# A two-layer hybrid backbone on one core: loads asked for earlier and in rooms of their own in the up projections, and context tiles beside two products of the first down projection

## The chip, the cores and the metric

The kernel runs on 1 core of one Trainium2 chip. The metric is the device time of the core in microseconds (us); the time of the kernel before is the median of 3 runs. The engines are PE (TensorE, matmuls), DVE (VectorE), ACT (ScalarE), POOL (GpSimd) and SP (SyncE, from whose queue every DMA of this kernel is issued).

## The reference

1024 latent tokens and 256 context tokens of width 1024 go through two layers. Each layer has a mixer (attention in layer 0, a gated recurrence in layer 1) and a convolutional feed-forward part, each modulated by rows that come from a conditioning vector (`ada_w`). Only the feed-forward part and those rows matter here:

```python
def conv_ffn(h, w_up, conv_w, conv_b, w_down):
    g, v = jnp.split(dwconv_centred(h @ w_up, conv_w, conv_b), 2, axis=-1)
    return (jax.nn.gelu(g, approximate=True) * v) @ w_down

mod_lat = (jax.nn.silu(c) @ ada_w[l] + ada_b[l])[:, None, :]
x = layer_norm(alpha * x + g1 * o_lat, ln1_g[l], ln1_b[l])
f_lat = conv_ffn(x * (1.0 + sc2) + sh2, ffn_w_up[l], ffn_conv_w[l], ffn_conv_b[l], ffn_w_down[l])
x = layer_norm(alpha * x + g2 * f_lat, ln2_g[l], ln2_b[l])
if not last:   # the same for the 256 context tokens
    f_ctx = conv_ffn(ctx * (1.0 + csc2) + csh2, ffn_w_up[l], ...)
```

The hidden width is 2816 = 22 blocks of 128. In layer 1 the context isn't needed after the mixer.

## The kernel before

All matmuls take three passes (`mm3`, lines 130 to 132): both operands are split into a high part (a cast on ACT, line 109) and a low part (a subtraction on DVE or POOL, line 110). Several large products are done with seven half-size products instead of eight (Strassen-Winograd); p1 to p7 are their names in the code.

**Up projection** (`ffn_up`, line 951). It goes over 22 channel blocks j. From j=3 on each j has the items p1, p2, (cg), p6, p5, p7, p3, p4, (cv); cg and cv are the context tokens' products, in layer 0 only. The weights of a j are two tiles of 512 KB, loaded into the ring `wr` of three buffers and split by `quarters` (line 940 forms their sums on POOL), four items ahead of use. Results leave the banks by copies on ACT and adds on DVE (lines 1059, 1075, 1078), go through a convolution along the tokens (`conv`, lines 895 to 898), GELU, and the product of gate and value (line 1087), and are stored as `g_s[j]`.

Beside this, a generator `more` is advanced by one step per item (not for cg and cv). In layer 0, `beside` (line 1165) first forms modulation rows (`ada`, 32 tiles of `ada_w`, one per step, each loaded into the ring `wr` and reduced by one DVE instruction at line 212) and then sums of layer 1's down weights (`down_sums`, 22 pieces: two loads of `w_dn`, four DVE subtractions at lines 380 to 386, two stores to `tw_s`; a piece lies in one `wr` buffer). In layer 1 `beside` does nothing.

From j=11 on, sums of the hidden values for the down projection (`sa_s`) are formed too (`more_sums`, lines 1108 to 1114): at item p1 of the next j, `g_s[j-11]` is loaded into lane 4, which is also the lane of the value convolution, and the four operations follow at p6, p5 and p7.

**Down projection** (`down`, line 1174). `run` goes over k blocks: it loads and splits a block of hidden values and a block of weights and does 12 matmuls. Banks 0 to 3 are set A, 4 to 7 set B. In layer 0 the two context tiles come first, alone, over all 22 k with weights 1024 wide; then p1 (A), p2 (B), p6 (A, on top of p1), p5 (B), p3 (B), p7 (A, on top), p4 (A, on top), 11 k each. `put` multiplies by the gate row, `norm` is the layer norm of a row tile, `modulate` transposes the result for the next block, as steps between the matmuls of the next `run` (`left`, `chain`). `fetch` loads a row tile of the residual and applies two DVE passes (lines 1191, 1195).

The order on each engine is that of the program, with a scheduler that may move an instruction ahead where the program leaves it free; matmuls with a key (`pe_key`) keep the program's order. An instruction that waits holds all behind it on its engine; the SP queue is such an engine for DMAs.

Of the kernel before, what the change touches and what calls it, by code (L numbers as in the profile page):

```python
# [58 lines left out]
class Kernel:  # L59
# [132 lines left out]
    def ada(self, pool, jobs, b):  # L192
# [8 lines left out]
        self.ld(bias, self.a["ada_b"])  # L201
        for l, part in jobs:
# [148 lines left out]
    def down_sums(self, pool, l, n):  # L351
# [3 lines left out]
        todo = [(k, c) for k in range(HF) for c in range(0, 512, n)]  # L355
# [16 lines left out]
        while have:  # L372
            if pool is None:
                yield
            k, view, x, y = have.pop(0)
            if pool is not None and todo:
                fetch()
                yield
# [4 lines left out]
            if pool is not None:  # L383
                yield
# [4 lines left out]
            if todo and not have:  # L389
                fetch()  # L390
                yield
# [559 lines left out]
    def ffn_up(self, l, nt, left, plain, lanes, jobs=()):  # L951
# [19 lines left out]
        with ExitStack() as es:  # L971
            self.spare((6, 7))
            more = self.beside(jobs)
# [59 lines left out]
            def finish(at, j, i):  # L1033
# [59 lines left out]
                end = j == KF - 1 and i == ends(j)  # L1093
                if len(both) == 1 and (i == "p1" or end):
                    f = lane(4)
                    self.ld(f[:, :TL], self.g_s[j - HF - (not end), :, :TL])
                    both.append(f)
                if not end:
                    more_sums(j - HF - 1, i)

            def more_sums(k, i):

                if len(both) < 2 or i not in ("p6", "p5", "p7"):
                    return
                g, f = both
                a11, a21, a12, a22 = f[:, :512], f[:, 512:TL], g[:, :512], g[:, 512:TL]
                if i == "p6":
                    nc.vector.tensor_add(a22, a21, a22)  # L1108
                elif i == "p5":
                    nc.vector.tensor_sub(a21, a11, a21)  # L1110
                    nc.vector.tensor_sub(a11, a22, a11)
                    self.st(self.sa_s[l, k, 1], f[:, :TL])
                else:
                    nc.vector.tensor_sub(a12, a12, a11)
                    self.st(self.sa_s[l, k, 0], g[:, :TL])
                    both.clear()

            sums, made_sums = iter(()), 0
            both = []
            for at, (j, i) in enumerate(seq):  # L1120
# [31 lines left out]
                if at >= begin + 8 and i not in ("cg", "cv"):  # L1152
# [4 lines left out]
            def rest():  # L1157
                for i in ("p6", "p5", "p7"):
                    more_sums(KF - 1 - HF, i)
                    yield  # L1160
# [3 lines left out]
    def beside(self, jobs):  # L1164


        if not jobs:
            return
        with ExitStack() as es:
            yield from self.ada(self.pool(es, "up", 1), jobs, 6)  # L1170
        yield from self.down_sums(None, 1, 256)


    def down(self, l, nt, x_in, x_out, nx, fold, norm_in, rest):
# [91 lines left out]

        A, B = ([(self.banks(i + s), None, i) for i in range(H)] for s in (0, 4))
        g, sa, tw = self.g_s, self.sa_s[l], self.tw_s[l]
        r1, r2 = half(0), half(1)
        if nt > NTL:  # L1270
# [3 lines left out]
            run(acc, KF, lambda k: g[k, :, TL:], lambda k: w[k], True, True, tiles)  # L1274
# [5 lines left out]
        self.spare((6, 7))  # L1280
        run(A, HF, lambda k: g[k, :, r1], lambda k: w[k][:, r1], True, False)
        p1, p5 = ([kept(n, u) for u in range(H)] for n in ("p1", "p5"))
        for o, _, u in A:
            nc.scalar.copy(p1[u], o)
        run(B, HF, lambda k: g[HF + k, :, r1], lambda k: w[HF + k][:, r1], True, True)
        for o, _, u in B:
            nc.vector.tensor_add(p1[u], o, p1[u])
            put(u, 0, p1[u])
        run(A, HF, lambda k: sa[k, 1, :, r1], lambda k: tw[k, 1, :, r2], False, False)
        p1 = [kept("p1", u) for u in range(H)]  # L1290
        for o, _, u in A:
            nc.scalar.copy(p1[u], o)
        run(B, HF, lambda k: sa[k, 0, :, r2], lambda k: tw[k, 0, :, r1], True, True,
            range(H if fold is not None else NTL))
# [558 lines left out]
```

## Time and profile before

| | |
|---|---|
| median of 3 runs | 2876.4 us (2875.54 to 2880.41) |
| the profiled execution's own time | 2875.91 us |
| its span, first to last instruction | 2872.9 us |
| mean granted clock of PE | 0.985 of 2.4 GHz |
| PE busy | 2745.3 us, 96% |
| DVE busy | 2172.5 us, 76% |
| ACT busy | 1526.6 us, 53% |
| POOL busy | 774.7 us, 27% |
| DMA | 493.48 MB, mean 172 GB/s |

Busy times are sums over instructions, as shares of the span; matmuls are pipelined, so their spans overlap. A granted clock of 1 is 2.4 GHz, and where a row shows less, part of its time was granted half of that. In the trace, layer 0's up projections with seven products per j run from about 1011 to 1528 us, its down projection from about 1515 to 1803 us, the recurrent block after it, layer 1's up projections from about 2200 to 2659 us, and its down projection to the end.

### The profile page before, as it was taken

What the parts mean: (1) busy time and instruction counts of PE and PEld (TensorE: products, weight loads), DVE (VectorE), ACT (ScalarE), POOL (GpSimd) and SP (SyncE); (2) the same over time, 40 slices, a digit from 0 to 9 for tenths busy, and PEclk for the clock granted to TensorE, in tenths of its full rate; (3) what the DMA queues carried; (4) which work ended last, traced back from release to release, by engine and by line L of the source; (5) the groups of instructions that cost most, each with busy time, mean ns of one, the idle gap of its engine ahead of it and who ended that gap; (6) DMA issues with size and microseconds to landing.
All of it is one profiled execution on the core that took longest, in us unless ns stands there. A gap on an engine that the chain in (4) does not pass through costs nothing.

```text
span 2872.9 us, 39350 instructions
## 1 busy us (share of the span) xinstructions
PE 2745.3 (96%) x14246; PEld 2273.4 (79%) x14246; DVE 2172.5 (76%) x3088; ACT 1526.6 (53%) x2490; POOL 774.7 (27%) x635
## 2 busy tenths in 40 slices
PE   7999999999999998999999999999989999999997
PEld 4877888888877877777887888788767888877885
DVE  6469878876666988778867758588787977877677
ACT  4222257777767643344444545577757544444444
POOL 4000002332100043444530001343211367762002
PEclk9999999999999999999999999999999999999998
DMA  7886875446175145446548667211264122446764
GB/s 291 323 265 242 278 221 122 96 114 145 62 268 197 48 165 183 167 165 225 174 144 285 209 198 241 89 52 58 73 232 152 59 89 88 140 155 219 256 217 165
DMA packets 197252, 493.48 MB, mean 172 GB/s; under 512 B 20382, under 2 KB 68542, under 8 KB 196930
## 3 DMA queue, kind: packets, MB, share of 16 engines
q1 hardware_dynamic: 197058, 490.98, 52.0%
q8 instruction: 111, 1.82, 0.3%
q14 instruction: 83, 0.68, 0.1%
HBM read 365.31 MB, written 125.59 MB: 171 GB/s over the span
## 4 chain that ended last, share of the span: by engine, by line
PE 38%; DVE 8%; DMA 5%; issue 3%; ACT 3%; POOL 1%; SPq 0%; DVEq 0%; ACTq 0%; POOLq 0%
PE pb L131 13%; PE pb L132 13%; PE pb L130 13%; DMA lane<-g_s 2%; DVE lane L898 1%; DVE lane L896 1%; DMA x<-x_s 1%; DVE lane L1087 1%; DVE wq L110 1%; DMA ar<-g_s 1%; DMA tw<-w_dn 1%; ACT lane L895 1%; POOL sq L940 1%; POOL wq L110 0%; DVE lane L1108 0%
## 5 line engine op out<-in xcount | busy, mean ns | idle before, releaser
L130 PE MATMUL pb<-hh,wh 128*128 128x512 f32 (+1 forms) x704 | 256.6, 365 | 8.2 <-ACT wh L109 8.0
L131 PE MATMUL pb<-hl,wh 128*128 128x512 f32 (+1 forms) x704 | 257.1, 365 | 0.4 <-DVE hl L731 0.4
L132 PE MATMUL pb<-hh,wl 128*128 128x512 f32 (+1 forms) x704 | 255.7, 365 | 1.0 <-DVE wl L110 1.0
L130 PE MATMUL pb<-wq,a 128*128 128x512 f32 x616 | 241.6, 392 | 6.2 <-ACT a L109 2.8
L131 PE MATMUL pb<-wq,a 128*128 128x512 f32 x616 | 240.8, 391 | 0.0
L109 ACT CAST a<-ar 128x512 fp32r<-128x512 f32 (+2 forms) x224 | 129.1, 580 | 191.3 <-PE pb L132 156.6
L110 DVE TENSOR_TENSOR wq<-wr,wq 128x512 fp32r<-128x512 f32 x262 | 203.3, 778 | 34.7 <-ACT wq L109 19.4
L110 DVE TENSOR_TENSOR a<-ar,a 128x512 fp32r<-128x512 f32 (+2 forms) x224 | 143.6, 644 | 103.6 <-ACT a L109 101.8
L940 POOL TENSOR_TENSOR sq<-wr 128x512 f32<-128x512 f32 x72 | 127.2, 1767 | 325.3 <-DMA wr<-w_up 268.5
L109 ACT CAST wq<-wr 128x512 fp32r<-128x512 f32 x262 | 161.5, 618 | 99.8 <-PE pb L132 62.8
L708 POOL TENSOR_SCALAR s<-s 128x1 f32<-128x1 f32 x36 | 21.7, 603 | 711.8 <-ACT x L707 711.4
L132 PE MATMUL pb<-wq,a 128*128 128x512 f32 x616 | 211.1, 391 | 0.0
L110 POOL TENSOR_TENSOR wq<-sq,wq 128x512 fp32r<-128x512 f32 x96 | 161.5, 1690 | 122.6 <-ACT wq L109 122.6
L130 PE MATMUL pb<-t,wq 128*128 128x512 f32 x400 | 161.4, 404 | 21.4 <-DVE lane L1075 12.5
L568 ACT ACTIVATE p<-pb,nm 128x1280 f32<-128x1280 f32 (+3 forms) x160 | 159.4, 999 | 40.2 <-DVE nm L1558 34.6
L131 PE MATMUL pb<-t,wq 128*128 128x512 f32 x400 | 160.0, 400 | 0.0
L132 PE MATMUL pb<-t,wq 128*128 128x512 f32 x400 | 159.7, 400 | 0.0
L109 ACT CAST wh<-wr 128x1024 fp32r<-128x1024 f32 x91 | 95.5, 1050 | 120.5 <-DMA wr<-w_qk 44.3
L130 PEld LDWEIGHTS pb<-hh,wh 128*128 128x128 f32 x704 | 133.7, 190 | 29.5 <-ACT wh L109 8.2
L110 DVE TENSOR_TENSOR wl<-wr,wh 128x1024 fp32r<-128x1024 f32 x91 | 111.0, 1220 | 58.6 <-ACT wh L109 57.6
L896 DVE SCALAR_TENSOR_TENSOR lane<-lane,cv 128x1023 f32<-128x1023 f32 x88 | 123.6, 1406 | 39.9 <-ACT lane L895 39.7
L131 PEld LDWEIGHTS pb<-hl,wh 128*128 128x128 f32 x704 | 133.7, 190 | 22.6 <-DVE hl L731 1.4
(357 smaller groups left out, 8135.1 us busy)
## 6 DMA issues: line engine op xcount, KB each, us to landing
wr<-w_up SPq DMA_DIRECT2D x88, 512.0 KB, 3.6
wr<-ada_w SPq DMA_DIRECT2D x80, 512.0 KB, 4.1
sa_s<-lane SPq DMA_DIRECT2D x44, 512.0 KB, 3.4
wr<-tw_s SPq DMA_DIRECT2D x88, 256.0 KB, 4.3
ar<-sa_s SPq DMA_DIRECT2D x88, 256.0 KB, 2.9
wr<-w_dn SPq DMA_DIRECT2D x66, 256.0 KB, 3.2
ar<-g_s SPq DMA_DIRECT2D x66, 256.0 KB, 4.0
wr<-w_ao SPq DMA_DIRECT2D x32, 512.0 KB, 7.1
```

The costliest lines, as they stand in the source:

```text
L109: self.cast = self.nc.scalar.copy(h, raw)
L110: return (sub or self.nc.vector).tensor_sub(l, raw, h.bitcast(F32))
L130: i = mm(out, a[0], b[0], start=first, stop=False, **kw)
L131: mm(out, a[0], b[1], start=False, stop=False, **kw)
L132: j = mm(out, a[1], b[0], start=False, stop=last, **kw)
L568: self.in_turn("att_act", self.nc.scalar.activation(*args, **kw))
L708: nc.gpsimd.tensor_scalar(rs, sq, 1.0 / D, EPS, op0=ALU.mult, op1=ALU.add)
L895: nc.scalar.activation(c, u, AF.Identity, scale=cvw[:, 1:2], bias=cvw[:, 3:4])
L896: nc.vector.scalar_tensor_tensor(c[:, 1:], u[:, :n - 1], cvw[:, 0:1], c[:, 1:], op0=ALU.mult, op1=ALU.add)
L898: nc.vector.scalar_tensor_tensor(c[:, :n - 1], u[:, 1:], cvw[:, 2:3], c[:, :n - 1], op0=ALU.mult, op1=ALU.add)
L940: op(have[n], x, y)
L1087: nc.vector.tensor_mul(g[:, :n], c.pop((j, 0))[:, :n], c.pop((j, 1))[:, :n])
```

## The change

In `ada` (with `apart`), a tile is asked for before the tile ahead of it is used, and every second tile gives one step more, so two tiles take three steps. In `down_sums`, `gap` sets how many steps lie between a load and its use (3 in layer 0, 4 in layer 1), and 9 of the 22 pieces of layer 1's weights move from layer 0's to layer 1's up projections, where they use a buffer of their own (`room`) and not the ring. The tile `f` for `more_sums` gets that room too; it is asked for at p3 of the same j instead of p1 of the next, and the operations come at p2, p6 and p5. In layer 0's down projection the context tiles no longer run alone: over the first 11 k they go with p1 and use the same split weights, over the other 11 k with p6; then p7, p2, p5, p3 and p4 follow. Layer 1's order stays.

```diff
-    def ada(self, pool, jobs, b):
+    def ada(self, pool, jobs, b, apart=False):
...
             for k in range(KD):
-                w = self.ring.tile([P, D], F32, name="wr", tag="wr")
-                self.ld(w, self.a["ada_w"][l, part, k])
+                w = have.pop(0) if have else turned(l, part, k)
+                if apart:
+                    at = jobs.index((l, part)) * KD + k + 1
+                    if at < len(jobs) * KD:
+                        have.append(turned(*jobs[at // KD], at % KD))
+                    if k % 2:
+                        yield
...
-    def down_sums(self, pool, l, n):
+    def down_sums(self, pool, l, n, part=slice(None), gap=0):
...
-            if pool is None:
-                xy = self.ring.tile([P, 2, 2, n], F32, name="tw", tag="wr")
+            if gap:
+                xy = (pool or self.ring).tile([P, 2, 2, n], F32, name="tw", tag="room" if pool else "wr")
...
-            if pool is None:
+            for _ in range(gap - 1):
                 yield
...
             self.st(view(self.tw_s[l, k, 0]), x)
-            if pool is not None:
-                yield
+            yield
...
             yield
-            if todo and not have:
+            if gap and todo:
                 fetch()
                 yield
...
-                end = j == KF - 1 and i == ends(j)
-                if len(both) == 1 and (i == "p1" or end):
-                    f = lane(4)
-                    self.ld(f[:, :TL], self.g_s[j - HF - (not end), :, :TL])
-                    both.append(f)
-                if not end:
+                if j >= HF and i == ("p3" if j < KF - 1 else ends(j)):
+
+                    f = room().tile([P, TL], F32, name="f", tag="room") if i == "p3" else lane(4)[:, :TL]
+                    self.ld(f, self.g_s[j - HF, :, :TL])
+                    other.append(f)
+                if j > HF:
                     more_sums(j - HF - 1, i)
...
-                if i == "p6":
+                if i == "p2":
                     nc.vector.tensor_add(a22, a21, a22)
-                elif i == "p5":
+                elif i == "p6":
...
-                if at >= begin + 8 and i not in ("cg", "cv"):
+                if at >= begin + 9 and i not in ("cg", "cv"):
                     next(more, None)
...
-        if not jobs:
-            return
-        with ExitStack() as es:
-            yield from self.ada(self.pool(es, "up", 1), jobs, 6)
-        yield from self.down_sums(None, 1, 256)
+        if l == 0:
+            with ExitStack() as es:
+                yield from self.ada(self.pool(es, "up", 1), jobs, 6, True)
+            yield from self.down_sums(None, 1, 256, slice(0, 13), 3)
+        else:
+            yield from self.down_sums(room(), 1, 256, slice(13, None), 4)
...
+        def with_ctx(acc, ctx, k0, a, b, fresh, want=()):
...
+            self.pe_key = f"dn{l}"
+            for k in range(HF):
+                parts = []
+                for src, cols in ((g[k0 + k, :, TL:], TC), (a(k), 512)):
...
+                    self.ld(ar[:, :cols], src)
+                    self.split(ar[:, :cols], hl[:, :cols], hl[:, 512:512 + cols])
+                    parts.append((hl, hl[:, 512:]))
+                wc = self.weight(w[k0 + k], (P, D), nc.vector)
+                wm = [x[:, r1] for x in wc]
+                if b is not None:
...
+                    self.ld(raw, b(k))
+                    self.split(raw, wq[:, 0], wq[:, 1])
+                    wm = wq[:, 0], wq[:, 1]
...
+                work = [(parts[0], wc, ctx, k0 + k == 0, k0 + k == KF - 1),
+                        (parts[1], wm, acc, fresh and k == 0, False)]
+                for x, ws, sums_, start, end in work if k0 + k < KF - 1 else work[::-1]:
...
         if nt > NTL:
...
-            run(acc, KF, lambda k: g[k, :, TL:], lambda k: w[k], True, True, tiles)
+            with_ctx(A, acc, 0, product[1][2], None, True)
+            p1 = copies("p1", A)
+            with_ctx(A, acc, HF, product[6][2], product[6][3], False, tiles)
+            p6 = copies("p6", A)
             for o, i, t in acc:
                 put(NTL + t, i, o)
             for t in tiles:
                 norm(t)
             left.append(self.modulate([ys[t] for t in tiles], NTL, fold))
...
+            run(*product[7])
...
+            run(*product[2], range(H))
+            second()
+            run(*product[5])
+            for o, _, u in B:
+                nc.vector.tensor_add(p5[u], o, p5[u])
+                nc.vector.tensor_add(p6[u], o, p6[u])
+            run(*product[3])
+            third()
...
+        run(*product[4], [t for t in range(H, NTL) if t not in xs],
+            KEEP if fold is not None else KEEP_LAST)
```

## Rows read from the trace of the kernel before

**Rows 1.** The page's first part: span, then each engine's busy us, share and instructions.

```profile
span 2872.9 us, 39350 instructions
PE 2745.3 (96%) x14246; PEld 2273.4 (79%) x14246; DVE 2172.5 (76%) x3088; ACT 1526.6 (53%) x2490; POOL 774.7 (27%) x635
```

**Rows 2.** Busy time by stretch; the first line names the columns.

```profile
core 0: us, PE busy (x) PEld busy (x) DVE busy (x) ACT busy (x) POOL busy (x), PEclk, DMA share, GB/s
1041.79:1404.34 362.55, 332.21 (x1677) 278.40 (x1677) 290.13 (x375) 144.22 (x219) 161.16 (x103) 0.97 0.56 185
1404.34:1502.66 98.32, 98.32 (x519) 83.96 (x518) 68.90 (x79) 45.60 (x67) 41.46 (x29) 1.00 0.40 138
1515.00:1560.00 45.00, 40.25 (x168) 31.80 (x167) 36.73 (x44) 20.60 (x28) 0.00 (x0) 0.96 0.89 309
...
1740.00:1770.00 30.00, 29.61 (x139) 24.12 (x137) 28.97 (x51) 20.70 (x32) 6.72 (x8) 1.00 0.80 284
1770.00:1803.00 33.00, 31.61 (x147) 26.20 (x148) 28.59 (x49) 14.44 (x24) 4.79 (x2) 1.00 0.65 215
1803.00:1840.00 37.00, 33.83 (x168) 26.16 (x167) 27.36 (x69) 20.53 (x27) 14.73 (x12) 1.00 0.28 98
2300.00:2440.00 140.00, 140.00 (x605) 113.38 (x604) 103.81 (x83) 66.65 (x100) 99.95 (x60) 1.00 0.26 90
...
2500.00:2640.00 140.00, 134.41 (x576) 107.34 (x575) 113.29 (x109) 63.03 (x96) 78.24 (x44) 1.00 0.47 163
```

**Rows 3.** Waits of PE, 1041.79 to 1404.34: releaser, total us, times, longest.

```profile
PE pb L130 <- DVE lane L1075: 16.3, 7, 4.4
```

**Rows 4.** Waits of DVE, 1041.79 to 1404.34.

```profile
DVE tw L380 <- DMA tw<-w_dn: 24.1, 10, 5.5
DVE wr L212 <- DMA wr<-ada_w: 14.1, 7, 6.1
...
DVE lane L1108 <- DMA lane<-g_s: 8.4, 4, 3.6
```

**Rows 5.** Groups of DVE, 1040 to 1400 (busy, mean ns); line 380 alone (min/median/max).

```profile
L212 DVE SCALAR_TENSOR_TENSOR wr<-wr,c_rows 128x1024 f32<-128x1024 f32 x26 | 37.9, 1458 | 14.5 <-DMA wr<-ada_w 14.1
L380 DVE TENSOR_TENSOR tw<-tw 128x256 f32<-128x256 f32 x22 | 16.4, 744 | 25.8 <-DMA tw<-w_dn 24.1 <-issue 1.7
...
L380 DVE TENSOR_TENSOR tw<-tw x22: 408/426/1522, 1150.1 to 1387.3; 128x256 f32<-128x256 f32 x22
```

**Rows 6.** Busy time by stretch, single j of layer 0 (store to store).

```profile
1064.39:1101.00 36.61, 32.60 (x154) 26.50 (x153) 26.49 (x33) 14.01 (x23) 19.70 (x12) 0.95 0.50 156
...
1268.65:1296.34 27.69, 27.64 (x143) 23.37 (x142) 21.45 (x29) 10.86 (x16) 11.88 (x8) 1.00 0.58 195
...
1348.23:1373.01 24.78, 24.61 (x130) 20.87 (x129) 22.55 (x28) 11.26 (x17) 10.81 (x8) 1.00 0.65 208
```

**Rows 7.** DMA issues (count, KB, median us to landing); SP queue's waits, 1041.79 to 1404.34.

```profile
sa_s<-lane SPq DMA_DIRECT2D x44, 512.0 KB, 3.4
...
SPq L89 <- DVE wr L212: 55.8, 23, 5.3
```

**Rows 8.** Waits of PE, 1500 to 1640; the chain of the whole run there (start, us).

```profile
PE pb L131 <- DVE wl L110: 4.5, 3, 2.1
...
1517.82 9.42 DMA ar<-g_s
```

**Rows 9.** Groups of DVE, 1740 to 1770.

```profile
L110 DVE TENSOR_TENSOR wq<-wr,wq 128x512 fp32r<-128x512 f32 x10 | 6.8, 682 | 0.0
...
L1191 DVE TENSOR_TENSOR x<-x,in 128x1024 f32<-128x1024 f32 x4 | 4.9, 1222 | 0.7 <-DMA x<-x_s 0.7
...
L1300 DVE TENSOR_TENSOR p<-pb,p 128x512 f32<-128x512 f32 x1 | 0.7, 681 | 0.0
```

**Rows 10.** Waits of DVE, 2300 to 2440, then 2500 to 2640.

```profile
DVE lane L896 <- ACT lane L895: 15.6, 10, 3.3
...
DVE lane L1108 <- DMA lane<-g_s: 10.7, 5, 4.3
```

**Rows 11.** Line 212 in one j: us, DVE busy (two instructions a tile), clock, DMA.

```profile
1101.00:1125.66 24.66, 9.19 (x12) 1.00 0.62 205
```

More of the change, by code (lines that the diff above doesn't have):

```diff
@@ L201, in ada, with turned @@
         self.ld(bias, self.a["ada_b"])
+        have = []
+        def turned(l, part, k):
+            w = self.ring.tile([P, D], F32, name="wr", tag="wr")
+            self.ld(w, self.a["ada_w"][l, part, k])
+            return w
         for l, part in jobs:
@@ L349, in sums @@
             yield
-    def down_sums(self, pool, l, n):
+    def down_sums(self, pool, l, n, part=slice(None), gap=0):
         sub = self.nc.vector.tensor_sub
-        todo = [(k, c) for k in range(HF) for c in range(0, 512, n)]
+        todo = [(k, c) for k in range(HF) for c in range(0, 512, n)][part]
         have = []
@@ L372, in down_sums @@
         while have:
-            if pool is None:
+            for _ in range(gap - 1):
                 yield
             k, view, x, y = have.pop(0)
-            if pool is not None and todo:
+            if not gap and todo:
                 fetch()
@@ L972, in ffn_up, with room @@
             self.spare((6, 7))
-            more = self.beside(jobs)
+            more, rooms = self.beside(l, jobs, lambda: room()), []
+            def room():
+                if not rooms:
+                    rooms.append(self.pool(es, "room", 1))
+                return rooms[0]
             making, made = {}, {}
@@ L1289, in down @@
[L1289 to L1294, printed above, removed]
-        for o, _, u in B:
-            nc.scalar.copy(p5[u], o)
-            nc.vector.tensor_add(p1[u], p1[u], p5[u])
-        run(B, HF, lambda k: sa[k, 0, :, r1], lambda k: w[HF + k][:, r2], True, True)
@@ L1299, in down @@
[L1299 to L1309 removed]
+            self.spare((6, 7))
@@ new lines, in down @@
+            run(*product[7])
+            p5 = [kept("p5", u) if u > 1 else gt[1][:, half(u)] for u in range(H)]
+            for o, _, u in A:
+                nc.scalar.copy(p5[u], o)
+            run(*product[2], range(H))
+            second()
+            run(*product[5])
+            for o, _, u in B:
+                nc.vector.tensor_add(p5[u], o, p5[u])
+                nc.vector.tensor_add(p6[u], o, p6[u])
+            run(*product[3])
+            third()
+        else:
+            self.spare((6, 7))
+            run(*product[1])
+            p1 = copies("p1", A)
+            run(*product[2])
+            second()
+            run(*product[6])
+            p6 = copies("p1", A)
+            run(*product[5], range(NTL))
+            for o, _, u in B:
+                p5[u] = kept("p5", u)
+                nc.scalar.copy(p5[u], o)
+                nc.vector.tensor_add(p6[u], p6[u], p5[u])
+            run(*product[3])
+            third()
+            run(*product[7])
+            for o, _, u in A:
+                nc.vector.tensor_add(p5[u], o, p5[u])
```

77 lines of the change are left out of this document (49 added, 28 removed).

## The prediction

> **What bounds the kernel now.** The first page part to read is the busy time: TensorE (PE) is busy 2745.3 of 2872.9 us, so all idle time of PE together is 127.6 us, and no edit that leaves the matmuls alone can be worth more than that and what the clock loses after a gap [rows 1]. The diff leaves every matmul in place: the same products over the same k. So the question is which part of the 127.6 us lies in the stages that it touches. The second view is the busy time by stretch [rows 2]; there the reader compares the length of a stretch with PE's busy time and looks at the granted clock. In layer 0's up projections, from channel block j=4 to j=16, PE is idle 362.55 - 332.21 = 30.3 us and the mean granted clock is 0.97, which costs another 0.03 x 362.55 = 10.9 us: 41 us in all. From j=17 to j=20, with no beside-work, PE is idle 0 and the clock is 1.00. Matmuls per us say the same (519 in 98.32 us against 1677 in 362.55 us, 0.189 us each: 317.7 us, so 45 us lost). The other stretches are small: the first 45 us of layer 0's down projection lose 4.75 us idle and 0.04 x 45 = 1.8 us of clock; layer 1's up projections lose nothing from 2300 to 2440 and 5.6 us from 2500 to 2640.
>
> Why PE stops in layer 0 is read next. The longest sum of its waits there is for VectorE's (DVE's) add at line 1075, 16.3 us, which empties a bank that the next product needs [rows 3]. DVE is busy 290 of 362.55 us, so it isn't full; but it works in order, and it stands still for loads that were asked for too late: 24.1 us for a piece of `w_dn` before line 380, 14.1 us for an `ada_w` tile before line 212, 8.4 us for `g_s` before line 1108 [rows 4]. 46.6 us of waiting on top of 290 us of work leaves 26 us of room in 362 us. That is why its adds come late.
>
> **The change part by part.**
>
> *Up projections of layer 0.* Work removed: none. The 32 `ada_w` tiles and four subtractions per piece keep their durations (1458 and 744 ns means) [rows 5]. Moved: the tiles go from one per step to two per three steps, each asked for one tile ahead; a piece is asked for three steps before it is used instead of one, and the pieces go from one per three steps to one per five. A step is one of seven items of a j, so a j takes about 25 us and a step 3.5 us, and the two waits for loads, 24.1 and 14.1 us, should end. The third, 8.4 us, should end too, since `f` is asked for at p3 and used at p2 of the next j. Per j, ada work falls from 7 x 1.46 = 10.2 to 6.8 us, and a third of the piece work goes (22 pieces to 13, of some 4 x 0.7 = 2.8 us). The last piece now lands near j=20 rather than j=15, so j=17 to j=20, which lose nothing today, get 1.4 x 2.8 = 3.9 us of DVE work on the 17 us of 24.6 that they have; that fits. What I take: 0.8 of the 41 us come back, **-33 us**. The bounds: all of it, -41; and, from the four j's that have pieces and sums together today (27.69 us the first, 24.78 the last; 1268.65 to 1373.01 is 26.1 on average, 1.5 over the undisturbed 24.6) [rows 6], if all 15 j's from 4 on with beside-work kept that loss: 22 left of 41, -19.
>
> The queue: `f`'s load at p3 waits in SP for the store of the sum that had the room before. That store is issued three items earlier (over 8 us) and lands in 3.4 us [rows 7], so nothing behind it (the `g_s` store, `w_up` of the next j) is held. It also frees lane 4, so the `value` convolution no longer waits for that store.
>
> *First down projection, start.* Today a k of the context tiles has 12 matmuls; PE waits 4.5 us in three pieces for the low half of a wide weight (line 110), with DVE's two passes over `x` in between, and the chain has a 9.42 us landing of `g_s` there, while gates, rows and `x` load too [rows 8]. Interleaved with p1 a k has 24 matmuls for one wide weight, so every load and split has twice the cover. Removed: 11 loads of 256 KB, 11 casts and 11 subtractions of 682 ns [rows 9], which no wait of PE in the middle of p1 rests on: worth 0. Added: a 256 KB load of `g_s` ahead of the first weight. Bounds: -6.5 (all the loss there) and +9.4 (one more landing like the one on the chain, uncovered). I take -3: the start of the stage is still crowded.
>
> *Copies of A.* ScalarE reads p1 and p6 out of bank set A while context matmuls run on B (12 of them, one k; p7 and p4 take 63 us for 22 k, so 2.9 us): the context goes first in the second half and last in its last k, which covers four copies. Cost 0; without that cover some 2 us each.
>
> *Order of the rest.* p2, p5, p3 now all accumulate in B. Between p2 and p5 and between p5 and p3 a bank is free after one and two DVE adds of 681 ns [rows 9]; the last k goes bank by bank, 0.7 us each, so PE waits at most 2 us, and I take **+1**. The other cost: p7 today stands between p3 and p4 and covers the norms of the first four row tiles, their modulation and the `x` loads of the next four. Now only p4 does. In the stretch of p7 and p4 DVE is busy 28.97 + 28.59 us of 63 [rows 2]; without p7's 22 splits of 0.68 us and four adds that is 57.6 - 15 - 2.7 = 40 us, of which some 5 fall after the last matmul, so 35 us must fit into the 31 us of p4 (half of 63). What is late next is then the modulated first half for the recurrent block, and its `x` passes of 1222 ns [rows 9]. Part of that delay falls into the 3.2 us that PE idles there anyway [rows 2]. Bounds 0 and +10 (9 us of the `x` passes and all of the modulation late); I take **+4**.
>
> *Up projections of layer 1.* Gain: the waits for `g_s` (10.7 us of DVE from 2500 to 2640) go [rows 10], and with them most of the 5.6 us: -4. Cost: nine pieces with four subtractions come to where DVE is busy 103.8 of 140 us (2300 to 2440) and PE loses nothing. At the 0.7 us of layer 0 they are 9 x 2.8 = 25 us on 36 us of room; of that room 15.6 us are waits of DVE for ScalarE [rows 10], partly usable. I take +3; bounds 0 and +16 (rival 2). Layer 1's own down projection keeps its order: 0.
>
> The Trainium skill speaks against this last part. The rows show a subtraction of 408 to 1522 ns in one shape, and GpSimd (POOL) busy 100 of 140 us in layer 1's stretch against 161 of 362.55 in layer 0's [rows 2, 5]. The page "SBUF — State Buffer", section "Who interferes with whom", states that a VectorE instruction with two inputs in SBUF contends with a GpSimd instruction that reads SBUF. By it the pieces would cost more in layer 1 than in layer 0; no row of before shows a piece there.
>
> **Sum.** -33 - 3 + 1 + 4 - 4 + 3 = -32 us. The profiled execution took 2875.9 us (span 2872.9 and 3.0 around it), the median of the three runs is 2876.4, so the two agree within 0.5 us, and the forecast is 2844 us.
>
> **The rivals.**
> 1. *The work, not the waits.* If DVE's in-order work as such makes its bank adds late, stretching it out moves the loss and doesn't remove it: layer 0 keeps its 41 us over more j's, and the rest of the sum (+1) stands: 2877 us. For it: j=12 and j=13 lose 3 us with the most work. Against: the 1348 to 1373 j has pieces and sums, DVE at 22.55 of 24.78 us, and loses 0.2 us [rows 6]. Chance 0.10.
> 2. *VectorE becomes the bound in layer 1.* If the subtractions take the longest measured time, 1.5 us, when POOL works beside them, nine pieces are 9 x 6.1 = 55 us on 36 us of room: 19 us over, in place of +3, and the sum is -16: 2860 us. For it: POOL's 71% and the 1522 ns. Against: the median in layer 0 is 426 ns [rows 5]. Chance 0.17. (The mechanism is the page's rule named above; the trace so far shows both prices.)
> 3. *The ring of three, slower than before.* `ada_w` tiles, pieces and `w_up` share the three `wr` buffers. Asking ahead keeps two of them for `ada_w`; if a `w_up` load then misses its lead of four items (some 11 us), PE stands in every j with `ada_w`. SP waits 55.8 us today for line 212 to free a buffer [rows 7], and one j took 36.61 us, 12 more than 24.6, with PE idle 4.0 us and the clock at 0.95 [rows 6]. Seven such j's are 84 us against the 22 us that j=4 to j=9 lose today; the sum without the 18 recovered there is -14, plus 62: +48, 2924 us. It decides from 7 us per j on. Against: the j from 1101 had six tiles in the same ring and took 24.66 us [rows 11]. Chance 0.08.
>
> **How the numbers follow.** Forecast 2844 us, chance 0.65; its own range, from the bounds of the terms (not all at one end together), is 2822 to 2860. The range that should hold takes in rival 2 with a margin for p4: 2822 to 2868; left out are rivals 1 and 3. A measurement of this kernel tells some 0.2% (5.8 us) from no change. Faster by more: 0.65 + 0.17, less 0.02 for a forecast that shrinks: 0.80. Within: rival 1, 0.10. Slower: rival 3 and a p4 that blocks the recurrent block, 0.10.
>
> **What would show it.** Right: from the store of j=3 to the store of j=20 in layer 0 about 430 us instead of 461, granted clock 1.00, DVE's waits for `w_dn` and `ada_w` under 10 us together; SP's wait for line 212 smaller. Start of the down projection: no wait of PE for line 110. p4 of layer 0: more PE idle time than 3 us around the start of the recurrent block. Layer 1: no wait of line 1108; DVE near 90% from 2300 to 2440 of the old time scale. Wrong: DVE waiting for loads as before, PE idle in each j of layer 0 with clock dips, or PE idle in layer 1 where it had none.

## The result and the profile after

The changed kernel takes 2899.8 us (median; 2896.4 to 2902.9), 1.0077 times the kernel before (95% interval 1.0054 to 1.0101): 0.8% slower, where 2844 us and 1% faster was forecast. The profiled execution took 2896.4 us. Its page begins:

```profile
span 2894.6 us, 39261 instructions
PE 2752.2 (95%) x14246; PEld 2278.0 (79%) x14246; DVE 2205.6 (76%) x3077; ACT 1519.5 (52%) x2479; POOL 788.4 (27%) x635
```

The matmuls are as many as before [rows 1]; PE's idle time went from 127.6 to 142.4 us, and its mean granted clock from 0.985 to 0.981. To see where, both runs are cut at the same stores (`g_s` of a j, the first and last `r_s` of the recurrent block). Busy time by stretch, first of before, then of after (length, PE, PEld, DVE, ACT, POOL, granted clock, DMA share, GB/s); in each block the lines are layer 0 from the third store to the eleventh, from there to the last, and the same for layer 1 (third to tenth, tenth to last):

```profile
1010.87:1242.12 231.25, 211.76 (x1061) 176.44 (x1060) 181.20 (x236) 93.52 (x143) 105.61 (x66) 0.97 0.51 170
1242.12:1528.13 286.01, 273.48 (x1404) 231.28 (x1402) 221.59 (x270) 123.80 (x184) 113.35 (x74) 0.99 0.56 190
2282.42:2416.31 133.89, 133.89 (x579) 108.44 (x578) 96.77 (x77) 64.98 (x97) 92.79 (x57) 1.00 0.23 81
2416.31:2659.03 242.72, 236.10 (x1014) 189.55 (x1013) 192.78 (x183) 113.64 (x172) 139.16 (x80) 1.00 0.47 163
```

```profile
1011.83:1227.44 215.61, 204.04 (x1041) 171.93 (x1039) 177.91 (x207) 92.35 (x141) 112.88 (x64) 0.98 0.45 150
1227.44:1508.40 280.96, 278.42 (x1441) 236.29 (x1440) 240.65 (x268) 125.55 (x187) 122.12 (x76) 1.00 0.55 187
2265.24:2428.25 163.01, 149.86 (x614) 118.95 (x613) 117.85 (x116) 66.43 (x101) 92.89 (x59) 0.96 0.40 132
2428.25:2674.75 246.50, 233.34 (x995) 185.74 (x994) 197.77 (x180) 109.22 (x165) 140.78 (x80) 1.00 0.44 151
```

Call the **loss** of a stretch its length less PE's busy time, plus (1 - granted clock) x length. The first line of before: 231.25 - 211.76 + 0.03 x 231.25 = 26.4 us. The same for all stretches and for the kernels of the experiments below, each from one profiled execution (the clock is given to 0.01 only, so a row of 360 us is good to some 2 us):

| loss, us | before | after | e1 | e2 | e6 | e9 | e14 | e17 | e18 | e20 |
|---|---|---|---|---|---|---|---|---|---|---|
| layer 0 up, 3rd to 11th store | 26.4 | 15.9 | 18.8 | 17.4 | 16.2 | 18.1 | 17.4 | 29.6 | 18.5 | 16.7 |
| layer 0 up, 11th to last | 15.4 | 2.5 | 27.5 | 8.2 | 3.9 | 3.9 | 0.8 | 0.9 | 0.8 | 3.8 |
| layer 0 down, to the first `r_s` | 9.2 | 22.9 | 22.0 | 11.5 | 22.9 | 8.4 | 16.5 | 15.1 | 30.2 | 8.1 |
| recurrent block and projections | 27.8 | 32.1 | 33.9 | 29.0 | 33.0 | 27.8 | 26.5 | 27.8 | 26.5 | 24.7 |
| layer 1 up, 3rd to 10th store | 0 | 19.7 | 0 | 23.0 | 1.4 | 5.5 | 6.3 | 6.0 | 5.0 | 4.4 |
| layer 1 up, 10th to last | 6.6 | 13.2 | 16.4 | 18.0 | 19.1 | 17.8 | 5.6 | 5.6 | 8.0 | 8.2 |
| layer 1 down | 27.8 | 30.2 | 32.1 | 29.3 | 30.6 | 33.1 | 30.4 | 27.3 | 29.6 | 30.1 |

Before to after: -10.5 - 12.9 + 13.7 + 4.3 + 19.7 + 6.6 + 2.4 = +23.3 us, against 21.7 us of span. Layer 0 gains 23.4; three places give back 40: the end of the first down projection and two stretches of layer 1. The two rows whose code is unchanged move by up to 9 and 6 us from kernel to kernel; nothing is concluded from that, and a difference of that size in a single row isn't an effect by itself.

**Place 1, p4 of layer 0.** Busy time by stretch there, three windows that answer to the last ones of layer 0 in [rows 2]; PE's waits from 1740 to 1840; and of PE's timeline the matmuls that come right after a wait (start, us, and in brackets the idle time ahead):

```profile
1740.00:1770.00 30.00, 25.26 (x115) 20.41 (x113) 28.34 (x44) 18.41 (x28) 12.34 (x10) 0.98 0.80 284
1770.00:1803.00 33.00, 26.04 (x95) 19.86 (x96) 24.51 (x48) 15.33 (x20) 6.81 (x10) 0.76 0.35 128
1803.00:1840.00 37.00, 34.35 (x174) 26.91 (x173) 19.33 (x50) 15.99 (x18) 8.50 (x4) 1.00 0.14 45
...
PE pb L131 <- DVE hl L743: 7.0, 5, 2.8
PE pb L132 <- DVE a L110: 3.8, 1, 3.8
...
1769.88 0.80 PE L132 MATMUL pb<-wq,a 128*128 128x512 f32 x1 [3.85 <-DVE a L110]
1782.43 0.50 PE L131 MATMUL pb<-hl,wh 128*128 128x512 f32 x1 [1.11 <-DVE hl L743]
```

Idle 4.74 + 6.96 + 2.65, clock 0.02 x 30 + 0.24 x 33: 22.9 us, where before lost 5.0 [rows 2]. `hl` is the low half of the modulated first row tiles, which the recurrent block multiplies; `a` is p4's own split. VectorE's timeline just ahead shows what the split stood behind, the `x` passes, and GpSimd's shows what ran beside it, the split of a wide weight:

```profile
1765.87 1.21 DVE L1212 TENSOR_TENSOR x<-x,in 128x1024 f32<-128x1024 f32 x1
1767.00 2.82 DVE L110 TENSOR_TENSOR a<-ar,a 128x512 fp32r<-128x512 f32 x1
1769.75 1.21 DVE L1216 TENSOR_TENSOR x<-x,in 128x1024 f32<-128x1024 f32 x1
...
1766.08 3.20 POOL L121 TENSOR_TENSOR wl<-wr,wh 128x1024 fp32r<-128x1024 f32 x1 [1.89 <-PE pb L738]
```

So the order is not all of this stop: the split takes 2.82 us, where the next one of the same form takes 0.68, and 2.1 of the 3.85 us are that. In before, GpSimd's splits of line 121 come later, from 1792.75 on. The two long waits for `hl`, 2.81 and 2.72 us, end behind other work of VectorE: six multiplications by the gate row (line 1221, from 1785.27) and three passes of the norms (line 717, from 1789.81).

**Place 2, the pieces in layer 1.** VectorE's timeline around two pieces (lines 393 to 398), and PE's first wait behind them:

```profile
2282.16 0.42 DVE L393 TENSOR_TENSOR tw<-tw 128x256 f32<-128x256 f32 x1
...
2283.61 0.43 DVE L397 TENSOR_TENSOR tw<-tw 128x256 f32<-128x256 f32 x1
2284.07 0.43 DVE L398 TENSOR_TENSOR tw<-tw 128x256 f32<-128x256 f32 x1
2290.22 0.42 DVE L393 TENSOR_TENSOR tw<-tw 128x256 f32<-128x256 f32 x1 [5.72 <-DMA tw<-w_dn]
...
2299.45 0.68 DVE L1094 TENSOR_TENSOR lane<-pb,m 128x512 f32<-128x512 f32 x1
...
2300.18 0.50 PE L130 MATMUL pb<-t,wq 128*128 128x512 f32 x1 [2.78 <-DVE lane L1094]
```

In the program four steps lie between a piece's load and its use. On VectorE the next piece stands directly behind the last one: the scheduler has moved the whole chain forward. The room is one tile, so the load can't start until the piece before is stored, and VectorE stands 5.72 us at the head of its queue with nothing able to pass. The splits and additions behind it are late, up to line 1094, which frees a bank for PE. VectorE's and PE's waits from 2265 to 2428:

```profile
DVE tw L393 <- DMA tw<-w_dn: 25.9, 7, 5.7
...
PE pb L130 <- DVE lane L1094: 9.7, 3, 3.9
```

**Place 3, the sums in layer 1.** From 2500 to 2680 the wait of [rows 10] for the load of `f` is gone, and the same addition (now line 1127) waits for something else, the store of the strip into which it writes. PE's longest sum of waits in this stretch, from 2428.25 on, is for p7's addition (now line 1094, 1075 before), which frees a bank; before, it waited for no addition there. VectorE's order has changed: before, the first addition of the sums stands behind p7's addition in all ten j's, in after ahead of it in eight. The waits of after, and one j of before:

```profile
DVE lane L1127 <- DMA g_s<-lane: 13.7, 6, 3.2
PE pb L130 <- DVE lane L1094: 5.3, 4, 1.6
...
2514.92 0.68 DVE L1075 TENSOR_TENSOR lane<-pb,m 128x512 f32<-128x512 f32 x1
2520.72 0.69 DVE L1108 TENSOR_TENSOR lane<-lane 128x512 f32<-128x512 f32 x1 [0.27 <-DMA lane<-g_s]
```

### The profile page after: what moved, and what is told of

It is laid out like the page before. It is cut to its first block, busy times and chain, and to the rows that moved or that the text cites. A ratio compares the mean times of both kernels' runs of the same rounds, so it can differ in the third digit from the quotient of the medians.

```text
span 2894.6 us, 39261 instructions
## 1 busy us (share of the span) xinstructions
PE 2752.2 (95%) x14246; PEld 2278.0 (79%) x14246; DVE 2205.6 (76%) x3077; ACT 1519.5 (52%) x2479; POOL 788.4 (27%) x635
## 5 line engine op out<-in xcount | busy, mean ns | idle before, releaser
L130 PE MATMUL pb<-wq,a 128*128 128x512 f32 x572 | 225.3, 394 | 4.8 <-DVE p L1401 3.0
L131 PE MATMUL pb<-wq,a 128*128 128x512 f32 x572 | 224.7, 393 | 0.0
L110 DVE TENSOR_TENSOR wq<-wr,wq 128x512 fp32r<-128x512 f32 x251 | 202.5, 809 | 20.3 <-ACT wq L109 17.2
L109 ACT CAST wq<-wr 128x512 fp32r<-128x512 f32 x251 | 155.4, 621 | 90.5 <-PE pb L132 68.9
L132 PE MATMUL pb<-wq,a 128*128 128x512 f32 x572 | 194.2, 393 | 3.8 <-DVE a L110 3.8
L130 PE MATMUL pb<-t,wq 128*128 128x512 f32 x400 | 159.9, 401 | 18.1 <-DVE lane L1094 14.5
L908 DVE SCALAR_TENSOR_TENSOR lane<-lane,cv 128x1023 f32<-128x1023 f32 x88 | 131.3, 1492 | 41.8 <-ACT lane L907 41.1
```

What stands on the lines that cost most here:

```text
L109: self.cast = self.nc.scalar.copy(h, raw)
L110: return (sub or self.nc.vector).tensor_sub(l, raw, h.bitcast(F32))
L130: i = mm(out, a[0], b[0], start=first, stop=False, **kw)
L131: mm(out, a[0], b[1], start=False, stop=False, **kw)
L132: j = mm(out, a[1], b[0], start=False, stop=last, **kw)
L908: nc.vector.scalar_tensor_tensor(c[:, 1:], u[:, :n - 1], cvw[:, 0:1], c[:, 1:], op0=ALU.mult, op1=ALU.add)
```

## The experiments

Theories at the start. A: layer 0 gained about what was forecast less some, and three separate losses of order took it back. Rivals: the nine pieces are simply too much work for VectorE in layer 1 (the prediction's second rival), or the shared weights of the context tiles cost by themselves.

**Undoing one part.** e1 gives all pieces back to layer 0 with one step between load and use; e2 restores the old order of the first down projection.

```
-            yield from self.down_sums(None, 1, 256, slice(0, 13), 3)
-        else:
-            yield from self.down_sums(room(), 1, 256, slice(13, None), 4)
+            yield from self.down_sums(None, 1, 256, slice(None), 1)
```

> The changed kernel with all 22 pieces of layer 1's down weights back in layer 0 (one step between load and use instead of three, so that they fit there), and none in layer 1. Theory A (the nine pieces in layer 1 cost what the two traces differ by between the stores of j=2 and j=7 there, 30 us): 2870 to 2880 us, with layer 0 a few us longer and layer 1 from 2300 to 2440 without idle time of PE. Rival (the loss in layer 1 comes from the sums in their room): within 5 us of the changed kernel's 2900.

> The changed kernel with the first down projection in the order of before (context tiles alone, then p1 p2 p6 p5 p3 p7 p4). Theory B (p4 alone can't cover the norms, the modulation and the residual passes; from layer 0's last store to the first store of the recurrent block the changed kernel takes 7.6 us more): 2890 to 2894 us, with PE idle under 3 us in p4 and its clock at 1.00. Rival (the interleaved context saves more at its start than p4 costs): 2900 us or more.

e1: 2904.4 us (ratio 1.0092, 1.0077 to 1.0107), a miss, and by its time inside the rival's range. By the stretch the rival falls: layer 1's early stretch loses nothing again (-19.7), and layer 0's late one loses 27.5 in place of 2.5, with VectorE waiting 15.8 us in eight pieces for `w_dn` there. So putting the pieces back gains nothing; since e1 also shortens the distance for all 22 pieces, it doesn't say what nine of them alone cost in layer 0. e2: 2887.9 us (1.0035, 1.0022 to 1.0048), 2 us under its theory's range: 12 us back by the medians, and 11.4 in the down projection. The profiled execution took 2892.9 us, and in it the other rows lose what that row gains; e9 and e18 below set the same two orders against each other again.

**Work or order in layer 1.** e6 keeps each piece's first subtraction, in layer 1 alone, behind the latest addition from a bank (`evac`, set at p2, p7 and p3); the work is the same. e7 keeps the subtractions and stores and takes the waits away: the nine pieces aren't loaded, the subtractions run on a scratch tile, and what is stored isn't the sums, so that layer 1's second factors are changed.

```
-            sub(w11, w12, w11)
+            i = sub(w11, w12, w11)
+            if pool is not None and gap:
+                self.after(i, self.evac)
```

> The changed kernel with one order added: in layer 1 the first subtraction of each of the nine pieces stays behind the last add of DVE that the program has ahead of it, so the scheduler can't move it up to where its load has just been asked for. Same work, same single room. Theory A1 (DVE stands still for the room's load, 25.9 us of waits): those waits fall under 8 us, and the time is 2878 to 2888 us. Rival A2 (the subtractions themselves fill DVE and slow POOL): within 6 us of 2900.

> The changed kernel; of the nine pieces in layer 1 the loads are left out, the 36 subtractions run on a scratch tile that waits for no DMA, and the stores take a tile that has long been there (so these parts of the summed weights are not computed). Theory A1 (waits): the loss in layer 1 between j=2 and j=7 falls from 30 us to under 10, time 2874 to 2884 us. Rival A2 (work): 2894 us or more.

e6: 2883.9 us (1.0025, 1.0014 to 1.0036), as theory A said; e7: 2888.6 us (1.0039, 1.0026 to 1.0052), between the two. In e6 VectorE is busy 116.9 of 147.8 us in the early stretch (after: 117.9 of 163.0), with seven of the nine pieces in it, and the loss falls from 19.7 to 1.4. The other two pieces fall into the late stretch, which loses 19.1; it loses 18.0 in e2, which has none there, and 16.4 in e1, which has no pieces in layer 1. VectorE's wait for the pieces in that stretch (2255 to 2410) is now

```profile
DVE tw L396 <- DMA tw<-w_dn: 0.3, 1, 0.3
```

So it is the place in the queue, not the work. e7 keeps 9.1 us of loss, with one wait of PE for a GpSimd split (3.2 us) and one for line 1087 (2.7); how the subtractions lead to them wasn't followed.

**Do the losses add?** e9 is e6 with the old down order of e2.

> The changed kernel with the down order of before and with the nine pieces' first subtractions kept behind the last addition from the banks. Theory A (two independent losses, the crowding at the end of the first down projection, about 11 us, and the place of the nine pieces in VectorE's order, about 15 us): they add, 2899.8 - 11 - 15 = 2874 us, between 2869 and 2879. Theory B (one loss that shows in two places, since each only moves the same VectorE work): no better than the better of the two alone, 2883 to 2888.

2874.7 us (0.9984, 0.9975 to 0.9994): they add, within a microsecond of the forecast.

**What in the new down order costs.** e12 and e13 put p7 back between p3 and p4 and leave the context tiles with p1 and p6 (e13 with the kept-back pieces). In this order the transposes of the context tiles' modulation go through two banks that p2 is filling, so part of p2's sums is changed; the instructions are the same ones.

```
-            run(*product[7])
...
             run(*product[2], range(H))
             second()
             run(*product[5])
...
             run(*product[3])
             third()
+            run(*product[7])
```

> The changed kernel with p7 of the first down projection put back between p3 and p4 (the context tiles still share weights with p1 and p6). Theory A (the 20 us lost in p4 come from the modulated first half having only p4 for cover): with p7 as more cover 9 to 13 us of it come back, 2887 to 2891, and TensorE's granted clock in p4 stays at 0.95 or above. Theory B (the loss comes from the context tiles, whose products leave the later split of data behind): within 3 us of the changed kernel, 2897 to 2903.

> The changed kernel with p7 put back between p3 and p4 and with the nine pieces' subtractions kept behind the last addition from the banks. Theory A (two independent losses, and the shared weights as such gain): 2899.8 - 15 - 13 = 2872, between 2867 and 2876, at or below the kernel before. Theory B (the shared weights cost by themselves): 2880 to 2885, as with the pinned subtractions alone.

e12: 2897.6 us (1.0059, 1.0044 to 1.0075); e13: 2882.0 us (1.0010, 0.9998 to 1.0021). By their times theory A missed, and both lie in theory B's ranges. In the stretch it held: the three windows of p4 lose 7.4 us in e12, where after loses 22.9, and the middle one has the clock at 1.00 and PE idle 0.76 us,

```profile
1770.00:1803.00 33.00, 32.24 (x151) 26.37 (x150) 22.60 (x43) 16.51 (x24) 13.23 (x12) 1.00 0.58 195
```

and the down projection loses 14.6 us (e13: 10.4) in place of 22.9. In e12 layer 1's two stretches lose 8.5 us more than after (23.7 + 17.7), with unchanged code there, which hides the gain; e13, with the pieces held, gains 1.9 us over e6 where 13 were expected, which the two intervals don't tell from nothing, and where the rest went wasn't found. That p7 as cover heals p4 is shown; what the shared weights are worth with that cover stays open, as the version that would tell (p7 there and the context tiles' modulation later) wasn't run.

e18 asks the other way: the new order put into the best kernel then known (e14, below).

> The kernel of 2862.4 us with the changed order of the first down projection back in. Theory A (that order costs 11 to 14 us by itself, at p4, whatever stands around it): 2872 to 2877, and the granted clock in p4 falls to about 0.75 again. Theory B (it cost only in company of the other losses): 2860 to 2866.

2871.1 us (0.9978, 0.9967 to 0.9989) against 2862.4: 8.7 us more, a microsecond under theory A's range; the down stretch is 13.8 us worse, the clock from 1780 to 1820 is 0.87, and PE's waits from 1700 to 1850 are those of place 1 again, with 3.8 us for p4's split, which takes 2.83 us beside a GpSimd split here too:

```profile
PE pb L131 <- DVE hl L745: 7.4, 5, 2.8
```

**The sums in layer 1.** First theory: the store wait is the loss. e11 emits the three steps one product later.

> The changed kernel with the three steps of the sums one product later each (after p6, p5 and p7 instead of p2, p6 and p5), so that the first addition comes later behind the store of the g strip in whose tile it writes. Theory A (the 13.7 us that VectorE stands before this addition in layer 1 are what j 9 to 21 lost there): 6 to 10 us less, 2890 to 2894. Theory B (the stretch is bounded by VectorE's own work or by other waits, and this wait only shows in it): within 3 us of the changed kernel, 2897 to 2903.

2897.9 us (1.0059, 1.0043 to 1.0076); VectorE's wait for the store is 14.1 us, in after 13.7: the scheduler put the addition where it had been, right behind the product that makes the strip. The run said nothing of the cause, only that a later place in the program is no later place on the engine. e15 and e16 take the wait itself away, with a tile of its own for the result, in layer 1 and in both layers.

```
+                        a22s.append(lane(4)[:, :512])
+                        nc.vector.tensor_add(a22s[0], a21, a22)
-                        nc.vector.tensor_add(a22, a21, a22)
```

> The same kernel of 2874.7 us, and in layer 1 the result of the first addition goes to a tile of its own instead of over the g strip, and the strip's second form is stored in two halves; nothing is reordered by hand. Theory A (the write in place is what waits): the 19.8 us that VectorE stands before this addition fall below 4 us, TensorE's 10.5 us of waits for p7's addition below 3 us, 2864 to 2868. Theory B (bounded by VectorE's work): the waits move elsewhere, 2872 to 2878.

> As the run with a tile of its own for the first addition, in both layers. Layer 0 loses only 3 to 4 us in the same stretch, so theory A gives 0 to 2 us less than that run, 2862 to 2868; theory B 2872 to 2878.

e15: 2872.9 us (0.9978, 0.9968 to 0.9988); e16: 2886.4 us (1.0031, 1.0019 to 1.0043), 13.5 worse than e15 and outside both ranges; layer 0's late stretch loses 13.7 in place of 3.8, not pursued. The theory of the store falls: e15's time is not told from e9's, VectorE no longer waits for the store, PE waits more, and the late stretch of layer 1 loses 21.9 us in place of 17.8. PE's waits in the late stretch in e9, then in e15 (line 1096 is p7's addition, which frees a bank):

```profile
PE pb L130 <- DVE lane L1096: 10.5, 7, 1.7
```

```profile
PE pb L130 <- DVE lane L1096: 14.6, 7, 3.0
```

VectorE's timeline says why. In e9 the addition 1129 stands ahead of 1096, with its wait:

```profile
2520.33 2.21 DVE L1108 TENSOR_TENSOR lane<-lane 128x1024 f32<-128x1024 f32 x1
2525.28 1.46 DVE L1129 TENSOR_TENSOR lane<-f,lane 128x512 f32<-128x512 f32 x1 [2.74 <-DMA g_s<-lane]
2526.66 0.68 DVE L1096 TENSOR_TENSOR lane<-pb,m 128x512 f32<-128x512 f32 x1
```

In e15 the wait is gone and the whole block of sums (1131 to 1141) stands ahead of 1096, which starts 8.5 us after the product of line 1108, against 6.3 in e9. The additions also take longer there (1.66 us in place of 0.69), so VectorE is busy 215.2 us in the stretch, against 199.0:

```profile
2522.76 2.20 DVE L1108 TENSOR_TENSOR lane<-lane 128x1024 f32<-128x1024 f32 x1
2525.00 1.66 DVE L1131 TENSOR_TENSOR lane<-f,lane 128x512 f32<-128x512 f32 x1
...
2530.69 0.69 DVE L1141 TENSOR_TENSOR lane<-lane,f 128x512 f32<-128x512 f32 x1
2531.30 0.68 DVE L1096 TENSOR_TENSOR lane<-pb,m 128x512 f32<-128x512 f32 x1
```

Second theory: the order. e14 is e9 with the first addition kept behind p7's (`self.after(m_, self.evac7)`) and the rest at p3 and p4, in both layers; e19 is the changed kernel with that alone.

> The kernel with the old down order and the kept-back pieces (2874.7 us), and in it the first addition of the sums kept in VectorE's order behind p7's addition from the bank, the other steps at p3. Theory A (in layer 1 this addition writes in place over the g strip, stands for the strip's store to be read out, and p7's addition, which frees a bank for TensorE, stands behind it): j 9 to 21 of layer 1 lose 7 to 10 us instead of 17.8, 2864 to 2868. Theory B (the stretch is bounded by VectorE's work, the wait is only where its idle time shows): 2872 to 2878.

> The changed kernel with nothing else than the first addition of the sums kept behind p7's addition, the other steps at p3. Theory A (its place in VectorE's order costs j 9 to 21 of layer 1 some 10 us by itself): 2886 to 2892. Theory B (it pays only where the pieces are kept back too, since both compete for the same gaps of VectorE): 2896 to 2902.

e14: 2862.4 us (0.9939, 0.9918 to 0.9959), under theory A's range; the late stretch of layer 1 loses 5.6 us, and no wait for 1096 is left in it. VectorE there, with 1096 3.8 us after that product (which starts at 2522.66):

```profile
2526.49 0.68 DVE L1096 TENSOR_TENSOR lane<-pb,m 128x512 f32<-128x512 f32 x1
2527.61 0.69 DVE L1129 TENSOR_TENSOR lane<-f,lane 128x512 f32<-128x512 f32 x1 [0.44 <-DMA g_s<-lane]
```

The additions still write in place and still wait for the store, 6.6 us in all; PE waits for none of what stands behind them now, and the order is that of before in all ten j's. (e14's expectation named the store and the order together; e15 separates them.) e19: 2883.0 us (1.0023, 1.0011 to 1.0035), 16.8 us under after by the medians and 3 us under theory A's range; the late stretch loses 4.1 us in place of 13.2, and where the rest of the 16.8 lies isn't shown.

**Which edit gained in layer 0.** e17 is e14 with the `ada` tiles as before, one per step and none ahead.

> The kernel of 2862.4 us (old down order, kept-back pieces, sums behind p7) with the ada tiles of layer 0 as before: one per step, none asked for ahead. Theory A (layer 0 gained by spreading the ada tiles): 8 to 15 us of it are lost again, 2870 to 2877, in j 2 to 10. Theory B (it gained by the pieces' later use and their fewer number, since VectorE still waits 20 us for ada tiles): 2859 to 2866, within 3.5 us of that kernel.

2871.3 us (0.9979, 0.9967 to 0.9991): 8.9 us lost, all of it in j 2 to 10 (29.6 against 17.4). Theory A. But VectorE's wait for the tiles is no longer without the asking ahead than with it; 1010 to 1240, e17, then e14:

```profile
DVE wr L224 <- DMA wr<-ada_w: 19.8, 13, 3.9
```

```profile
DVE wr L224 <- DMA wr<-ada_w: 22.6, 14, 3.7
```

The wait that the asking ahead was to end is as long with it. That leaves the spacing, two tiles in three steps, as what helped; no run has one without the other, so this is argued and not shown. The rest of layer 0's gain, 23.4 - 8.9 = 14.5 us by the difference, is left for the pieces' later use and smaller number. e1 bears that out: with the tiles spaced as in the change and all 22 pieces one step from their loads, layer 0's two stretches lose 46.3 us, where before lost 41.8.

**The best version.** In e14 the down stretch of layer 0 lost 16.5 us against e9's 8.4; its sums stand later in layer 0 too. e20 has them behind p7 in layer 1 alone.

> The kernel of 2862.4 us (old down order, kept-back pieces, sums behind p7) with the sums of layer 0 put back to where the changed kernel has them, so that only layer 1's stand behind p7. Theory A (in layer 0 the later sums reach into the start of the down projection and cost there what they don't gain before): 2855 to 2861. Theory B (the place of the sums gains in layer 0 as in layer 1): 2864 to 2869.

2855.8 us, ratio 0.9928 (0.9905 to 0.9950): inside theory A's range, and faster than before and than the change. From e14 its time isn't told apart (the intervals overlap); the down stretch does lose 8.1 us again. Its page and its two stretches of layer 1:

```profile
span 2851.4 us, 39327 instructions
PE 2736.2 (96%) x14246; PEld 2268.6 (80%) x14246; DVE 2215.0 (78%) x3088; ACT 1523.0 (53%) x2490; POOL 782.7 (27%) x635
...
2251.87:2394.81 142.94, 139.94 (x595) 112.36 (x594) 112.80 (x106) 64.06 (x98) 89.45 (x57) 0.99 0.38 127
2394.81:2628.56 233.75, 227.93 (x968) 181.55 (x967) 201.44 (x185) 109.43 (x166) 137.14 (x80) 0.99 0.48 164
```

VectorE is busier than in after, 2215.0 against 2205.6 us, in a run 43 us shorter.

## Why the prediction was wrong

- **Up projections of layer 0, -33.** The loss went from 41.8 to 18.4 us: -23.4, inside the bounds and near the weak one. The step that failed is "the two waits for loads, 24.1 and 14.1 us, should end". That for `w_dn` nearly did [rows 4]; that for `ada_w` grew. VectorE's waits in after, j=4 to j=20, and the longest one of the SP queue:

```profile
DVE wr L224 <- DMA wr<-ada_w: 20.2, 14, 3.4
DVE tw L393 <- DMA tw<-w_dn: 6.2, 3, 5.1
...
SPq L89 <- DVE wr L224: 53.3, 25, 5.3
```

  The SP queue stands as long for line 224 to free a buffer as it did before, 53.3 against 55.8 us [rows 7]: a load that is asked for one tile ahead, into a ring whose buffers are all in use, started no sooner here. (The piece work falls by 9 of 22, two fifths, where the prediction says a third.) The duration named was right: from the store of j=3 to that of j=20, 1044.94 to 1479.66, 434.7 us, against 430 forecast and 461 before.
- **Start of the down projection, -3.** Right in size. 1500 to 1545 loses 1.8 us, where before lost 6.5 [rows 2]; PE still waits for line 110, 1.8 us in two from 1500 to 1640, where the forecast's sign was no wait:

```profile
1500.00:1545.00 45.00, 43.17 (x190) 35.10 (x189) 32.00 (x39) 16.17 (x24) 0.00 (x0) 1.00 0.70 234
```

- **Copies of A, 0, and B after B, +1.** PE is busy 150.00 of 150 us from 1590 to 1740, and 70.00 of 70 from 1520 to 1590: 0 and 0.
- **p4 as the only cover, +4.** The mechanism was the one named (the modulated half late behind VectorE's other work), the size was not: 22.9 - 5.0 = +18 us in the windows, beyond the bound of +10; put into or taken out of a kernel the order is worth 8.7 to 12 us (e18, e2, e9). Two steps failed. The sum compared VectorE's total work with the length of p4, 35 against 31 us, and not the order: an `x` pass whose result is wanted last stood ahead of p4's own split, so PE stopped inside p4 too (3.8 us). It also took p4's splits at the 0.68 us of [rows 9], where this one took 2.82 beside GpSimd's. And it left out the clock: after these waits the mean granted clock was 0.76 from 1770 to 1803, 8 of the 18 us. What each would cost alone wasn't separated.
- **Waits for `g_s` in layer 1, -4.** It came to +6.6 us. The wait named did go; the step that failed is that what goes would not come back. With the load asked for sooner, the scheduler placed the addition sooner, right behind the product and in eight of ten j's ahead of p7's addition; e11, with the three steps as late as before, has the same order. The bare wait was not the cost (e15), the place was (e14, e19).
- **Nine pieces in layer 1, +3.** It was +19.7, beyond the bound of +16. The second rival had the size, 19 over, by another mechanism: VectorE was not full (117.9 of 163 us; the forecast's sign for the mechanism, near 90%, is absent: 72%), and e6 has the same work at a loss of 1.4. The failed step is reading "asked for four steps before it is used" in the program and taking it for VectorE's order. Kept in place, the pieces leave that stretch a loss of 1.4 to 7.0 us in the nine runs that do it: the +3 was about right for the order that the program writes.
- **Rivals 1 and 3.** Layer 0 did recover, and from j=4 on no j takes over 30.2 us, where before had one of 36.6 [rows 6] and rival 3 wanted seven: both fall. Slower came about by three terms that were sized too small (p4, the `g_s` waits, the pieces), not by either.

The page's rule of the prediction can now be weighed. The nine pieces' four lines take 774, 829, 660 and 528 ns in the mean in layer 1, 698 ns together, against 680 ns for the thirteen in layer 0 and 687 for the 22 before (744 is the first line alone [rows 5]): dearer in layer 1 by nothing that counts. Single instructions do show two prices, 0.43 us at 2283.61, with no GpSimd work beside it, and 1.50 us for the same line when a GpSimd split runs:

```profile
2302.51 1.50 DVE L397 TENSOR_TENSOR tw<-tw 128x256 f32<-128x256 f32 x1
2302.39 2.75 POOL L110 TENSOR_TENSOR wq<-sq,wq 128x512 fp32r<-128x512 f32 x2 [3.95 <-ACT wq L109]
```

So the trace agrees for single instructions with the rule of the Trainium skill ("SBUF — State Buffer", "Who interferes with whom"). It decides nothing in layer 1's stage.

In e20 the sum reads: layer 0 up -21.3, its down -1.1, the middle -3.1, layer 1 up +6.0, its down +2.3, together -17.2 us by the losses against 21.5 us of span (the clock is given to 0.01 only, which is 1 us in 100). The gain in layer 0 was real, and most of what was lost elsewhere came back by changing the order on one engine; in p4 that order also decided which of VectorE's instructions ran beside GpSimd's.

## What to carry to other kernels

On an engine that works in order, ask of every new instruction that waits for a transfer which instruction stands behind it and whether another engine needs that one: work that fits into the idle time by its sum can still cost several times what the sum says (19.7 us in place of 3). Where a scheduler may move instructions forward, a distance written in the program ("four steps after the load") isn't a distance on the engine: tie work that nobody waits for behind the instruction that frees a bank. And a wait that the profile names is a symptom: take it away and see if the engine that sets the end gets faster, before it is called the cause.

## What the runs showed of the hardware

A few short gaps of PE cost twice here. In p4 and the recurrent block's start PE waited 3.85, 1.11, 2.81 and 2.72 us within 25 us. After the first of these, and again after the third, the granted clock was 0.50, the lower of its two levels (1.2 GHz), from 1770 to 1775 and from 1790 to 1795, and matmuls took 0.63 us in place of 0.39; from 1780 to 1785 it was back at 1.00. The mean over the 33 us was 0.76. The wait of 2.78 us in place 2 was followed by matmuls of 0.63 us too, with the clock at 0.66 from 2300 to 2305. In the late stretch of layer 1, where waits of at most 3.0 us lie spread over 246 us, the mean stayed at 1.00; in e15, with more of them there (14.6 us in seven, the longest 3.0), it was 0.97. The prediction's sum had no term for this.
